# Two blocks of a transformer: large tiles in SBUF moved to multiples of 128 bytes

## The chip, the cores and the metric

The kernel runs on one core of a Trainium2 chip. The metric is the time of one execution in device microseconds; a median of several runs is given. The profile is of one further execution.

## What is computed

Two different blocks are applied one after the other to one sequence of 256 tokens with a width of 2048, all in fp32. The reference, cut to its products:

```python
def first_block(x, ...):
    h = rms_norm(x, norm1_w[l])
    proj = h @ w_in[l]                          # 2048 x 10792
    o_nsa = nsa_mixer(q, nsa_kv, nsa_g, ...)    # sparse attention, 8 heads
    o_dn = gated_deltanet(dn_qkv, dn_z, ...)    # 8 heads, chunks of 64
    mixed = g_nsa * (o_nsa @ w_up_nsa[l]) + g_dn * (o_dn @ w_up_dn[l])
    x = x + mixed @ w_o[l]
    h2 = rms_norm(x, norm2_w[l])
    x = x + (silu(h2 @ w_ffn_gate[l]) * (h2 @ w_ffn_up[l])) @ w_ffn_down[l]
    return rms_norm(x, norm_f_w)

def second_block(x, ...):
    h = rms_norm_2(x, attn_norm_g[l])
    proj = h @ w_in[l]
    y_rwkv = rwkv7_mixer(h_r, h_k, h_v, ...)    # a recurrence over the tokens
    y_mla = mla_mixer(c_q, c_kv, k_pe, ...)     # latent attention
    x = x + concatenate([y_rwkv, y_mla]) @ w_out[l]
    h = rms_norm_2(x, ffn_norm_g[l])
    x = x + conv_glu_ffn(h, w_gate, w_up, conv_w, conv_b, w_down)
    return rms_norm_2(x, final_norm_g)
```

Both feed-forward blocks are 5632 wide. The weights, 476 MB, are read once.

## The kernel before

Every large product is made of f32r matmuls on operands split in two parts: `hi` is the value rounded to f32r, `lo` the rest. Three products of parts (hi hi, hi lo, lo hi) are added in PSUM. The weights come as pieces of 128 x 1024 numbers (512 KB) into one of five `wraw` buffers (`wchunks`); ScalarE makes `whi` from a piece (line 294) and VectorE `wlo` (line 295), three buffers each. The activations are split once and stay in SBUF.

There are two kinds of product. In `gemm_tok` (token-major) the activation is the stationary operand, 128 tokens at a time, and the weights are the moving one, 512 columns, in a few places 256. `mm3` issues a triple for each k and each half of the tokens: stationary hi with `whi`, stationary hi with `wlo`, stationary lo with `whi`. In `gemm_feat` (feature-major) the weights are stationary and the activation is moving. Its hi and lo parts of 256 tokens each lie behind each other, so that one matmul of 512 columns takes both with `whi`; one of 256 columns takes the hi part with `wlo`. For a piece of four k there are eight wide matmuls and then eight narrow ones.

```python
def mm3(self, o, a, b, start, stop):          # gemm_tok
    self.mm(o, a[0], b[0], start, False)
    self.mm(o, a[0], b[1], False, False)
    self.mm(o, a[1], b[0], False, stop)
...
for k, (wh, wl) in piece:                     # gemm_feat, wide
    for m in range(nm):
        self.mm(ps[:, m].rearrange("p i t -> p (i t)"), wh[:, ms[m]], X.wide(xk0 + k), k == 0, False)
...
for k, (wh, wl) in piece:                     # gemm_feat, narrow
    for m in range(nm):
        self.mm(ps[:, m, 0], wl[:, ms[m]], X[0][:, xk0 + k], False, k == kt - 1)
```

The order of the work is fixed when the program is built: `weave` lays the products and the steps of the mixers beside each other by a table of costs (`Pace`), and the recording helper gives almost every instruction the line 131. So instructions go by their tiles. A row names out<-moving,stationary: `mmA<-whi,se` is a matmul of gemm_tok with the activation `se` stationary, `mmA<-hh,whi` one of gemm_feat with the activation `hh` moving. `pB` is the output of the mixers' small matmuls.

The stages in order of time: block 1's projections and mixers (gemm_feat on `sbc`, the gates `z` with gemm_tok), the gates and products that merge them, `w_o` (gemm_tok on `sbc`), gate and up of the feed-forward block (gemm_feat on `sde`), down (gemm_tok on `sbc`, which then holds the first 16 of 44 k, and on `hidh` and `hidl`); block 2's projections (gemm_feat and gemm_tok on `sde`) with its mixers, the latent attention's projections (`sd`), the output projection (gemm_tok, first on `se`, then on `sa`), gate and up (gemm_feat on `hh`), down (gemm_tok, on `sa` for hi and `se` for lo of the first 16 k, then on `hidh` and `hidl`; the last 512 columns as two groups of 256).

Where a tile lies: tiles are laid out once, when the program is built, pool by pool, from below and, for the pools of the right side, from above. `cpool` (constants) comes first, then `wpool` (weights), `hpool` (slot `sa`), `npool` (small tiles and `xn`), then the pools of the stages. `pad0` and `pad1` are tiles of 32 bytes that nothing reads or writes; `pad0` puts the weights' buffers at multiples of 128 bytes. Within a tile every operand of a large product begins a multiple of 512 bytes behind the tile's start, so it has the tile's remainder.

Of the kernel before, what the change touches and what calls it, by code (L numbers as in the profile page):

```python
# [9 lines left out]
F32 = mybir.dt.float32  # L10
# [8 lines left out]
P = 128  # L19
# [99 lines left out]
class Traced:  # L119


    def __init__(self, pace, key):
        self.pace, self.key, self.eng = pace, key, getattr(pace.nc, key)
# [104 lines left out]
class Kern:  # L228
    def __init__(self, tc, A, out, ctx):
        self.tc, self.nc, self.A, self.out, self.ctx = tc, Pace(tc.nc), A, out, ctx  # L230
        self.cpool = ctx.enter_context(tc.tile_pool(name="cpool", bufs=1))

        self.cpool.tile([P, 8], F32, name="pad0")
        ctx.enter_context(tc.tile_pool(name="rpool", bufs=1, side="right")).tile([P, 8], F32, name="pad1")
        self.wpool = ctx.enter_context(tc.tile_pool(name="wpool", bufs=3))
        self.hpool = ctx.enter_context(tc.tile_pool(name="hpool", bufs=1))
        self.npool = ctx.enter_context(tc.tile_pool(name="npool", bufs=2))
        self.psA = ctx.enter_context(tc.tile_pool(name="psA", bufs=2, space=PSUM))
        self.psB = ctx.enter_context(tc.tile_pool(name="psB", bufs=4, space=PSUM))
        self.ident = self.cpool.tile([P, P], F32, name="ident")  # L240
        self.prm = self.cpool.tile([P, NPARAM], F32, name="prm")
        self.cst = None
        self.sides = ctx.enter_context(ExitStack())
        self.new_side()
        self.later = []
# [1677 lines left out]
```

## Time and profile before

| | before |
|---|---|
| median of 3 runs | 2783.31 us (2782.2 to 2783.56) |
| the profiled execution, its own time | 2780.21 us |
| its span, first to last instruction | 2778.4 us |
| mean granted clock of TensorE | 0.998 |
| TensorE busy | 2733.4 us, 98% |
| VectorE, ScalarE, GpSimd busy | 1828.6, 1334.3, 224.6 us |
| read from HBM | 476.30 MB, 173 GB/s over the span |

A busy time counts an engine as busy from the start of an instruction to its end. TensorE's matmuls are pipelined: one begins long before the last has ended, so what a matmul costs is the distance from its start to the next one's. In a timeline, where equal instructions that follow each other stand in one row, that distance is read from the starts of rows and the counts between them.

### The profile page before, as it was taken

To read this page: it belongs to the slowest core of one execution; us is meant where nothing else is said; L and a number is where in the kernel's file an instruction comes from. 1 tells how busy PE (TensorE), PEld (TensorE's weight loads), DVE (VectorE), ACT (ScalarE), POOL (GpSimd) and SP (SyncE) were. 2 spreads that over 40 slices of the span, in tenths; PEclk is the share of its full clock that TensorE was granted. 3 is DMA by queue.
4 is the path that set the end of the run, shared out by engine and by line. 5 is a ranking of instruction groups with operands and counts; after the bars stand their busy time and mean duration, and the time that the engine had idled before them with its cause. 6 is when DMAs were issued, how large, how long until landed. Compare 5 with 4: busy or idle time off the path is not lost.

```text
span 2778.4 us, 39888 instructions
## 1 busy us (share of the span) xinstructions
PE 2733.4 (98%) x15536; PEld 2342.9 (84%) x15536; DVE 1828.6 (66%) x2590; ACT 1334.3 (48%) x1775; POOL 224.6 (8%) x253
## 2 busy tenths in 40 slices
PE   9999999999999999999999999999999999999998
PEld 8987888888788888888888877878888888888888
DVE  7788769866565565564555787776576677675454
ACT  5556545454454444443444544445354444444433
POOL 0000000001000000000001321110000000000000
PEclk9999999999999999999999999999999999999999
DMA  7643465555656665565555643332556666665554
GB/s 243 205 144 106 130 190 167 173 162 181 218 185 191 193 192 190 190 191 188 192 195 183 199 121 107 109 89 105 199 179 192 190 191 191 193 189 189 188 188 143
DMA packets 418655, 484.15 MB, mean 174 GB/s; under 512 B 26113, under 2 KB 343297, under 8 KB 417826
## 3 DMA queue, kind: packets, MB, share of 16 engines
q1 hardware_dynamic: 415808, 475.94, 53.8%
q10 hardware_dynamic: 2658, 5.66, 0.6%
q8 instruction: 122, 2.00, 0.3%
q14 instruction: 67, 0.55, 0.1%
HBM read 476.30 MB, written 5.24 MB: 173 GB/s over the span
## 4 chain that ended last, share of the span: by engine, by line
PE 87%; DVE 4%; POOL 1%; ACT 1%; issue 1%; DMA 0%; ACTq 0%; DVEq 0%; POOLq 0%
PE mmA L131 78%; PE pB L131 8%; DVE wlo L295 1%; DVE iw L131 1%; POOL sd L131 0%; ACT whi L294 0%; DVE ar L131 0%; DVE sd L131 0%; DVE MM L131 0%; DVE xn L131 0%; DMA wA<-in_rwkv_w_dram 0%; POOL psb L131 0%; POOL xn L131 0%; DVE X L131 0%; DVE bt L131 0%
## 5 line engine op out<-in xcount | busy, mean ns | idle before, releaser
L295 DVE TENSOR_TENSOR wlo<-wraw,whi 128x1024 fp32r<-128x1024 f32 x889 | 1092.9, 1231 | 768.1 <-ACT whi L294 754.0
L294 ACT CAST whi<-wraw 128x1024 fp32r<-128x1024 f32 x889 | 928.1, 1045 | 1168.1 <-PE mmA L131 1001.6
L131 PE MATMUL mmA<-sde,whi 128*128 128x512 f32 (+1 forms) x1888 | 468.2, 387 | 1.1 <-DVE sde L131 1.1
L131 PEld LDWEIGHTS mmA<-sde,whi 128*128 128x128 f32 x1888 | 334.5, 188 | 56.4 <-DVE sde L131 1.3
L131 PE MATMUL mmA<-hh,whi 128*128 128x512 f32 x1408 | 351.8, 392 | 0.0
L131 PE MATMUL mmA<-sbc,whi 128*128 128x512 f32 (+1 forms) x1216 | 304.4, 383 | 2.0 <-ACT whi L294 1.5
L131 PEld LDWEIGHTS mmA<-hh,whi 128*128 128x128 f32 x1408 | 251.5, 188 | 43.2
L131 PEld LDWEIGHTS mmA<-sde,wlo 128*128 128x128 f32 x1840 | 249.2, 188 | 20.4 <-DVE wlo L295 1.7
L131 PE MATMUL mmA<-sde,wlo 128*128 128x256 f32 x1840 | 261.5, 279 | 1.5 <-DVE wlo L295 1.5
L131 PEld LDWEIGHTS mmA<-sbc,whi 128*128 128x128 f32 x1216 | 212.5, 188 | 35.8 <-ACT whi L294 2.6
L131 PE MATMUL mmA<-whi,sbc 128*128 128x512 f32 (+1 forms) x768 | 234.4, 379 | 0.6 <-DVE xn L131 0.6
L131 PEld LDWEIGHTS mmA<-hh,wlo 128*128 128x128 f32 x1408 | 188.2, 188 | 14.6
L131 PE MATMUL mmA<-hh,wlo 128*128 128x256 f32 x1408 | 191.5, 278 | 0.0
L131 PE MATMUL mmA<-whi,hidh 128*128 128x512 f32 (+1 forms) x504 | 186.5, 370 | 0.0
L131 PE MATMUL mmA<-wlo,hidh 128*128 128x512 f32 (+1 forms) x504 | 186.5, 370 | 0.0
L131 PE MATMUL mmA<-whi,hidl 128*128 128x512 f32 (+1 forms) x504 | 186.5, 370 | 0.0
L131 PE MATMUL mmA<-sbc,wlo 128*128 128x256 f32 x1152 | 172.6, 281 | 1.4 <-DVE wlo L295 1.4
L131 PEld LDWEIGHTS mmA<-sbc,wlo 128*128 128x128 f32 x1152 | 158.8, 188 | 14.7 <-DVE wlo L295 1.8
L131 PEld LDWEIGHTS mmA<-whi,sbc 128*128 128x128 f32 x768 | 142.0, 188 | 29.6 <-DVE xn L131 0.8
L131 PE MATMUL mmA<-wlo,sbc 128*128 128x512 f32 (+1 forms) x384 | 144.8, 377 | 0.6 <-DVE wlo L295 0.6
L131 POOL TENSOR_TENSOR sg<-sg,rb 128x512 f32<-128x512 f32 x44 | 68.1, 1547 | 579.2 <-ACT sg L131 579.2
L131 PEld LDWEIGHTS mmA<-whi,hidl 128*128 128x128 f32 x504 | 95.2, 189 | 17.8
(440 smaller groups left out, 3242.9 us busy)
## 6 DMA issues: line engine op xcount, KB each, us to landing
wraw<-in_w_in_dram SPq DMA_DIRECT2D x232, 512.0 KB, 3.5
wraw<-in_w_ffn_gate_dram SPq DMA_DIRECT2D x88, 512.0 KB, 3.4
wraw<-in_w_ffn_up_dram SPq DMA_DIRECT2D x88, 512.0 KB, 3.5
wraw<-in_w_ffn_down_dram SPq DMA_DIRECT2D x88, 512.0 KB, 4.2
wraw<-in_ffn_w_gate_dram SPq DMA_DIRECT2D x88, 512.0 KB, 3.5
wraw<-in_ffn_w_up_dram SPq DMA_DIRECT2D x88, 512.0 KB, 3.6
wraw<-in_ffn_w_down_dram SPq DMA_DIRECT2D x88, 512.0 KB, 3.4
wraw<-in_w_o_dram SPq DMA_DIRECT2D x32, 512.0 KB, 3.6
```

Source lines behind the costliest of these rows:

```text
L131: r = f(out, *a, **k)
L294: nc.nc.scalar.copy(h, r)
L295: nc.nc.vector.tensor_sub(l, r, h.bitcast(F32))
```

## The change

`pad1` grows from 32 to 96 bytes, and a new tile of 64 bytes, `pad2`, stands first in `npool`. Nothing uses either.

```diff
         self.cpool.tile([P, 8], F32, name="pad0")
-        ctx.enter_context(tc.tile_pool(name="rpool", bufs=1, side="right")).tile([P, 8], F32, name="pad1")
+        ctx.enter_context(tc.tile_pool(name="rpool", bufs=1, side="right")).tile([P, 24], F32, name="pad1")
         self.wpool = ctx.enter_context(tc.tile_pool(name="wpool", bufs=3))
         self.hpool = ctx.enter_context(tc.tile_pool(name="hpool", bufs=1))
         self.npool = ctx.enter_context(tc.tile_pool(name="npool", bufs=2))
+        self.npool.tile([P, 16], F32, name="pad2", bufs=1)
```

Everything from `npool` upwards moves up by 64 bytes, everything on the right side moves down by 64. No instruction is added, removed or moved. The start of some tiles in a partition, in bytes, and its remainder by 128, as the two built programs have them:

```
tile                          before            after
wraw, whi, wlo (11 buffers)   19072 ... 60032    the same     0 ->  0
sa                            64128              64128        0 ->  0
xn (3 buffers)                80512 ... 84608    + 64         0 -> 64
sbc, hh                       88256              88320       64 ->  0
hidh                         121024             121088       64 ->  0
hidl                         149696             149760       64 ->  0
se, sde                      196544             196480       64 ->  0
cst (block 1)                121600             121664        0 -> 64
ar, km, bt (block 2)         130560 ... 148992   + 64         0 -> 64
X, XT, Lo, Y (block 2)       159296 ... 173696   + 64        64 ->  0
```

`sa` is 16 KB long. The matmuls of f32r by the remainders of their operands' starts (moving, stationary), counted in the built programs:

```
columns  matmuls  before    after
512      4544     (64, 0)   (0, 0)    gemm_feat, wide
512      2616     (0, 64)   (0, 0)    gemm_tok
512       384     (0, 0)    (0, 0)    gemm_tok on sa
256      5132     (64, 0)   (0, 0)    gemm_feat, narrow, and short ones
256       688     (0, 64)   (0, 0)    gemm_tok, narrow
256       128     (0, 0)    (0, 0)    gemm_tok on sa, narrow
```

Of the fp32 matmuls of the mixers, 375 have a stationary operand that goes from 64 to 0, and 256 one that goes from 0 to 64.

## Rows read from the trace of the kernel before

**Rows 1.** The page: busy time by engine, and TensorE's granted clock in 40 slices.
```profile
PE 2733.4 (98%) x15536; PEld 2342.9 (84%) x15536; DVE 1828.6 (66%) x2590; ACT 1334.3 (48%) x1775; POOL 224.6 (8%) x253
...
PEclk9999999999999999999999999999999999999999
```

**Rows 2.** The page's chain that ended last; waits: who for whom, us, times, longest.
```profile
PE 87%; DVE 4%; POOL 1%; ACT 1%; issue 1%; DMA 0%; ACTq 0%; DVEq 0%; POOLq 0%
...
ACT whi L294 <- PE mmA L131: 1001.6, 633, 8.2
```

**Rows 3.** Stretches: from:to us, busy time by engine (instructions), clock, DMA, GB/s.
```profile
8.00:782.00 774.00, 764.46 (x4475) 652.21 (x4476) 571.50 (x884) 415.66 (x596) 41.20 (x50) 1.00 0.56 174
782.00:1269.00 487.00, 487.00 (x2832) 428.94 (x2831) 288.34 (x296) 233.79 (x271) 39.34 (x22) 1.00 0.60 191
...
1518.00:2034.00 516.00, 494.04 (x2992) 417.93 (x2990) 377.53 (x730) 248.67 (x410) 88.23 (x117) 0.99 0.43 136
...
2521.00:2778.00 257.00, 246.31 (x1320) 210.80 (x1319) 121.37 (x120) 97.49 (x106) 15.09 (x9) 0.99 0.51 176
```

**Rows 4.** Timeline of TensorE, output projection on `se`: start us, us, matmul, count.
```profile
1948.70 0.39 PE L131 MATMUL mmA<-wlo,se 128*128 128x512 f32 x1
1948.94 0.63 PE L131 MATMUL mmA<-whi,se 128*128 128x512 f32 x2
...
1971.81 0.39 PE L131 MATMUL mmA<-wlo,se 128*128 128x512 f32 x1
```

**Rows 5.** Timeline of TensorE, output projection on `sa`.
```profile
1990.63 0.39 PE L131 MATMUL mmA<-wlo,sa 128*128 128x512 f32 x1
...
2010.35 0.39 PE L131 MATMUL mmA<-wlo,sa 128*128 128x512 f32 x1
```

**Rows 6.** Timeline of TensorE, down projection of block 2: mixed triples, then `hidh`, `hidl`.
```profile
2524.72 0.40 PE L131 MATMUL mmA<-whi,se 128*128 128x512 f32 x1
...
2542.75 0.40 PE L131 MATMUL mmA<-whi,se 128*128 128x512 f32 x1
2542.98 0.39 PE L131 MATMUL mmA<-whi,hidh 128*128 128x512 f32 x1
...
2546.48 0.40 PE L131 MATMUL mmA<-whi,hidh 128*128 128x512 f32 x1
```

**Rows 7.** Timeline of TensorE, the same projection's groups of 256 columns, mixed triples.
```profile
2704.96 0.28 PE L131 MATMUL mmA<-whi,sa 128*128 128x256 f32 x1
...
2709.55 0.28 PE L131 MATMUL mmA<-whi,sa 128*128 128x256 f32 x1
```

**Rows 8.** Groups of instructions by shape: count, busy us, mean ns of one, idle before.
```profile
L131 PE MATMUL mmA<-whi,hidh 128*128 128x512 f32 x392 | 155.0, 396 | 0.0
...
L131 PE MATMUL mmA<-whi,sa 128*128 128x512 f32 x224 | 77.4, 390 | 0.0
...
L131 PE MATMUL mmA<-whi,hidh 128*128 128x256 f32 x112 | 31.5, 281 | 0.0
...
L131 PE MATMUL mmA<-whi,sa 128*128 128x256 f32 x64 | 18.0, 281 | 0.0
...
L131 PEld LDWEIGHTS mmA<-whi,hidh 128*128 128x128 f32 x504 | 94.7, 188 | 17.8
...
L131 PEld LDWEIGHTS mmA<-whi,sa 128*128 128x128 f32 x288 | 54.1, 188 | 8.9
```

**Rows 9.** Timeline of TensorE, gate and up of block 2: wide and narrow matmuls in turn.
```profile
2300.28 2.00 PE L131 MATMUL mmA<-hh,whi 128*128 128x512 f32 x8
2302.11 1.07 PE L131 MATMUL mmA<-hh,wlo 128*128 128x256 f32 x8
2303.02 1.99 PE L131 MATMUL mmA<-hh,whi 128*128 128x512 f32 x8
2304.85 1.11 PE L131 MATMUL mmA<-hh,wlo 128*128 128x256 f32 x8
2305.79 0.39 PE L131 MATMUL mmA<-hh,whi 128*128 128x512 f32 x1
```

## Prediction

> **What bounds the kernel now.** I read the page's busy shares first. [...] Second, the chain that ended last: 87% of it is TensorE [rows 2]. Third, who waits for whom: ScalarE's split of the weights waits 1001.6 us in all for TensorE to give a `whi` buffer back [rows 2], so the weights are ahead of TensorE and not behind. Fourth, the stretches: in the gate and up products of the first feed-forward block TensorE has no idle time at all (487.00 of 487.00 us); its idle time lies in the mixers and at the end [rows 3]. So the time is the sum of the distances from the start of one matmul to the start of the next. A row's own duration (some 390 ns for 512 columns) overlaps its neighbours'; only the distance counts.
>
> The change adds, removes and moves no instruction: on every engine the two programs' lists agree word for word but for tile numbers and line numbers, waits included. What differs is where tiles begin. So each term is a number of matmuls times a difference in distance that belongs to an address.
>
> **The token-major products (gemm_tok).** Here the activation is the stationary operand and the weights, which lie at 0 of 128 before and after, are the moving one. The trace of before holds both cases of the stationary operand. In the output projection of block 2, first half, it is `se`, at 64 of 128: from 1948.70 to 1971.81 us there are 33 triples of matmuls, 23.11 us, so 700 ns a triple, 233.4 each [rows 4]. In the second half it is `sa`, the one large tile that lies at 0 of 128: from 1990.63 to 2010.35 us there are 29 triples, 19.72 us, so 680 ns a triple, 226.7 each [rows 5]. Code, weights, width and engines' load are alike in the two halves. In the down projection of block 2 both kinds of tile stand in one triple (two `sa`, one `se`): 18.03 us for 26 triples, 693.5 ns; directly after it `hidh` and `hidl`, both at 64, need 3.50 us for 5, 700 ns [rows 6]. The difference follows the tile and changes within a quarter microsecond, so it is not the stage's.
>
> The count, from the loops: the down projection of block 1 has 4 x 44 x 2 = 352 triples, `w_o` 128, the two `z` gates 64, the two latents 64, the first half of the output projection 64, and the down projection of block 2 3 x 28 x 2 = 168: 840 triples at 700 ns. They go to 680: 840 x 20 ns = **16.8 us less**. The 96 mixed triples go from 693.5 to 680: **1.3 us less**. The down projection's last two groups are 256 columns wide, and there the alignment shows nothing: mixed triples with `sa` take 4.59 us for 13, 353 ns or 117.7 each [rows 7], and the mean duration is 281 ns whether the stationary operand is `sa` or `hidh`, while at 512 columns it is 390 against 396 [rows 8]. The weight loads themselves last 188 ns in either case [rows 8], so the gain is not in the load's length. I cost the narrow ones at nothing.
>
> **The feature-major products (gemm_feat).** Here the weights are stationary, at 0 of 128, and the activation is moving, at 64 of 128 before and at 0 after. No row of before has this product with a moving operand at 0, so I bound it. A stretch of the second feed-forward block shows eight matmuls of 512 columns and then eight of 256, in turn: 1.83 us for the eight wide ones (2300.28 to 2302.11), 228.8 each; 0.91 and 0.94 us for the narrow ones, 113.8 and 117.5 by turns, 115.6 on average [rows 9]. The loops give 4544 wide and 4544 narrow ones (2816 in the feed-forward blocks, 1728 in the mixers).
>
> Wide: the nearest row with both operands at 0 is the `sa` triple, 226.7 [rows 5]. That gives 2.1 x 4544 = 9.5 us less. At the other end nothing changes. I take the row: **9.5 us less**. Narrow: the two levels that stand by turns are the bounds. All at 113.8 would be 1.8 x 4544 = 8.2 us less, all at 117.5 1.9 x 4544 = 8.6 us more. The nearest row with both operands at 0 is the triple of 256 columns, 117.7 [rows 7], so I take the upper one: **8.6 us more**. These two terms nearly cancel, and both are weaker than the first.
>
> **The other operands.** The small fp32 matmuls of the mixers read some tiles that move from 64 to 0 and some that move from 0 to 64 (`cst`, `ar`, `bt`, `km` among them): of their stationary operands 375 go to 0 and 256 leave it. At the 6.7 ns of the wide products that would be 2.5 us less and 1.7 us more; they are 256 columns or narrower with few exceptions, where rows 7 and 8 show no difference, so I take 0. The `xn` tiles move from 0 to 64, read and written by VectorE and ScalarE; these have 34% and 52% of the span free [rows 1], and that slack hides it. If it were gone, TensorE would idle for longer where it waits for these engines now, in the mixers: there it idles 22 us of 516 in block 2 [rows 3]. A faster TensorE asks the weights' transfers for under 1% more; the 1001.6 us of waiting [rows 2] cover that.
>
> **Sum.** 16.8 + 1.3 + 9.5 - 8.6 = 19.0 us less; all but the idle stretches pass it on, so I take 18. The profiled execution took 2780.21 us by its own time, 3.1 under the median of the runs, 2783.31: it would become 2762, and the median 2765. Bounds of this case: 18.1 + 9.5 + 8.2 = 35.8 us less, and 18.1 - 8.6 = 9.5 us less, or 2747 to 2774.
>
> **Rivals.**
> First, `sa` is fast for where it lies and not for its alignment: its 16 KB begin where the weights' buffers end. Then the triples stay at 700 ns, and only the uncertain terms are left, which nearly cancel: about 2783. For it: `sa` is the only large activation at 0, so the trace can't part the two. Against it: the nearest of the slow ones, `hidh`, begins 40 KB behind the end of `sa`, and `se` 113 KB, and both run at 700, so between these two the place makes no difference [rows 4, 6].
>
> Second, no offset counts that is a multiple of something smaller than 64. Then `sa` and `se` would not differ, and the time stays at 2783. Rows 4 to 6 speak against it directly; what is left is that `sa` differs in some way I don't see. [...]
>
> Third, slower: in gemm_feat the two operands now lie at the same phase, where before they lay half of 128 apart, and they may get in each other's way when the next weights load beside the running matmul. If the wide ones then take what a bad pair takes elsewhere, 233.4 instead of 228.8, that is 20.9 us more; with all narrow ones at 117.5, 8.6 more: 29.5 - 18.1 = 11.4 us more, 2795. It decides where a wide and a narrow one together lose more than 18.1 us / 4544 = 4.0 ns. Against it: in the `sa` triples both operands are at 0 too, and those are the fastest rows of this width.
>
> That the change doesn't do what it says can be left out: the built program's addresses show every large activation at 0 of 128.
>
> **Numbers.** My forecast 0.78, the first rival 0.10, the second 0.05, the third 0.07. A measurement of this kernel tells about 0.2% from no change, 5.6 us; the whole range of the forecast is beyond that. So faster 0.78, same 0.15, slower 0.07. The range is the forecast's own, 2747 to 2774, carried up to 2780 to take in the rivals' nearer side.
>
> **What would show it.** Right: triples of 680 ns in both down projections and in `w_o`, wide ones of 226 to 227 ns in gemm_feat, unchanged busy times of VectorE and ScalarE. The first step is wrong if `hidh` triples still take 700 ns; the second if the wide ones of gemm_feat stay at 228.8; the third if the narrow ones go to 113.8 throughout (a larger gain), or beyond 117.5. The forecast is wrong as a whole if TensorE's sum falls and idle time before it grows by as much.

## The result: slower by 0.6%

The changed kernel takes 2799.88 us (median of 5 runs, 2797.68 to 2800.9) against 2782.41 us for the kernel before (5 runs beside them): a ratio of 1.0062, interval 1.0051 to 1.0073. That is 17.5 us more where 18 less were forecast. The two profiled executions stand 20.2 us apart (2780.21 and 2800.45), their spans 20.3 (2778.4 and 2798.7).

The page of the changed kernel, busy times, clock and chain, answers to [rows 1, 2]:

```profile
PE 2756.3 (98%) x15536; PEld 2363.0 (84%) x15536; DVE 1834.4 (66%) x2590; ACT 1334.4 (48%) x1775; POOL 219.5 (8%) x253
...
PEclk9999999999999999999999999999999999999999
...
PE 89%; DVE 3%; ACT 1%; issue 0%; POOL 0%; DMA 0%; ACTq 0%; SPq 0%; DVEq 0%; POOLq 0%
```

TensorE's count of instructions is the same, its mean granted clock nearly so (0.998 before, 0.996 after), and it is busy 22.9 us longer; its idle time fell a little (2778.4 - 2733.4 = 45.0 us before, 2798.7 - 2756.3 = 42.4 after). So nothing waits longer: the matmuls themselves lie further apart. The stretches say where. First the gate and up products of block 2 in the kernel before (busy us and instructions of PE, PEld, DVE, ACT, POOL; then clock, DMA share, GB/s):

```profile
2034.00:2521.00 487.00, 487.00 (x2831) 428.57 (x2830) 343.36 (x435) 234.78 (x275) 30.78 (x42) 1.00 0.60 190
```

Then the changed kernel, the stretches of [rows 3] with the one just shown ahead of the last:

```profile
8.00:789.00 781.00, 773.88 (x4475) 659.68 (x4476) 576.27 (x883) 416.61 (x596) 36.84 (x50) 1.00 0.55 172
789.00:1282.00 493.00, 493.00 (x2829) 433.92 (x2828) 288.20 (x295) 232.48 (x271) 39.28 (x22) 1.00 0.59 188
...
1529.00:2046.00 517.00, 495.69 (x2998) 420.96 (x2996) 378.26 (x731) 248.75 (x410) 87.78 (x117) 0.99 0.43 136
2046.00:2542.00 496.00, 496.00 (x2831) 432.77 (x2829) 344.60 (x435) 234.39 (x276) 30.62 (x42) 1.00 0.59 186
2542.00:2797.00 255.00, 245.55 (x1322) 211.91 (x1321) 121.35 (x120) 97.96 (x106) 15.07 (x9) 0.99 0.52 177
```

The two feed-forward stages of gemm_feat have become longer, block 1's (on `sde`) by 6 us and block 2's (on `hh`) by 9; block 1's projections and mixers (gemm_feat on `sbc`) by 7. Block 2's down projection, gemm_tok, is 1 us shorter: from its first matmul to its last it takes 245.2 us where it took 246.2 (its stretch above ends 1.7 us before the span does, that of [rows 3] 0.4). That is the forecast's sign for gemm_tok, at less than its size, and the opposite sign for gemm_feat.

Single rows show it by tile. TensorE's timeline in the changed kernel, as in [rows 4 to 7]: first and last `wlo` row of unbroken triples on `se`, mixed triples, `hidh` and `hidl`, and mixed triples of 256 columns:

```profile
1960.50 0.40 PE L131 MATMUL mmA<-wlo,se 128*128 128x512 f32 x1
...
1994.54 0.39 PE L131 MATMUL mmA<-wlo,se 128*128 128x512 f32 x1
...
2542.29 0.40 PE L131 MATMUL mmA<-wlo,sa 128*128 128x512 f32 x1
...
2563.41 0.39 PE L131 MATMUL mmA<-wlo,sa 128*128 128x512 f32 x1
2564.11 0.40 PE L131 MATMUL mmA<-wlo,hidh 128*128 128x512 f32 x1
...
2599.65 0.40 PE L131 MATMUL mmA<-wlo,hidh 128*128 128x512 f32 x1
...
2724.61 0.28 PE L131 MATMUL mmA<-wlo,sa 128*128 128x256 f32 x1
...
2734.69 0.28 PE L131 MATMUL mmA<-wlo,sa 128*128 128x256 f32 x1
```

`se`: 50 triples in 34.04 us, 681 ns, 226.9 a matmul, where it was 233.4: as forecast. Mixed: 31 triples in 21.12 us, 681 ns: as forecast. But `hidh` and `hidl`: 51 triples in 35.54 us, 697 ns, 232.3 a matmul. They begin at 0 of 128 just as `se` does, and have gained one nanosecond. The narrow mixed triples went up, from 353 ns to 360 (28 in 10.08 us).

The timeline of gate and up, [rows 9]'s view, in the changed kernel, of block 1 on `sde` and of block 2 on `hh`:

```profile
1000.06 2.00 PE L131 MATMUL mmA<-sde,whi 128*128 128x512 f32 x8
1001.90 1.12 PE L131 MATMUL mmA<-sde,wlo 128*128 128x256 f32 x8
1002.86 2.00 PE L131 MATMUL mmA<-sde,whi 128*128 128x512 f32 x8
...
2311.64 2.02 PE L131 MATMUL mmA<-hh,whi 128*128 128x512 f32 x8
2313.49 1.10 PE L131 MATMUL mmA<-hh,wlo 128*128 128x256 f32 x8
2314.43 2.03 PE L131 MATMUL mmA<-hh,whi 128*128 128x512 f32 x8
2316.30 1.12 PE L131 MATMUL mmA<-hh,wlo 128*128 128x256 f32 x8
2317.26 2.02 PE L131 MATMUL mmA<-hh,whi 128*128 128x512 f32 x8
```

Eight wide ones on `sde` take 1.84 us (230.0 each), eight narrow ones 0.96 (120.0). On `hh` the wide ones take 1.85 and 1.87 us (232.5), the narrow ones 0.94 and 0.96 (118.8). Both are slower than before (228.8 and 115.6), and they differ from each other, though both tiles are at 0 of 128.

What divides the tiles stands in the table of tile starts ahead of the prediction, if it is read modulo 256 and not 128. The weights begin at 19072, 128 above a multiple of 256, in both kernels. Before, `sbc` and `hh` (88256), `hidh`, `hidl` and `se`, `sde` all began 64 bytes behind the weights' phase; `sa` (64128) at the same phase. After, `se` and `sde` (196480) have the weights' phase, distance 0; `sbc`, `hh` (88320), `hidh` (121088) and `hidl` (149760) lie 128 away, half a period. A multiple of 128 can be either. In what follows the **distance** is the start of the activation's operand minus that of the weights' operand, modulo 256.

### The profile page after: what moved, and what is told of

It is laid out like the page before. It is cut to its first block, busy times and chain, and to the rows that moved or that the text cites. A ratio compares the mean times of both kernels' runs of the same rounds, so it can differ in the third digit from the quotient of the medians.

```text
span 2798.7 us, 39888 instructions
## 1 busy us (share of the span) xinstructions
PE 2756.3 (98%) x15536; PEld 2363.0 (84%) x15536; DVE 1834.4 (66%) x2590; ACT 1334.4 (48%) x1775; POOL 219.5 (8%) x253
## 4 chain that ended last, share of the span: by engine, by line
PE 89%; DVE 3%; ACT 1%; issue 0%; POOL 0%; DMA 0%; ACTq 0%; SPq 0%; DVEq 0%; POOLq 0%
PE mmA L131 81%; PE pB L131 8%; DVE wlo L296 1%; DVE iw L131 0%; DVE ar L131 0%; DMA cst<-in_consts_dram 0%; DVE MM L131 0%; ACT whi L295 0%; DVE sd L131 0%; POOL psb L131 0%; POOL xn L131 0%; DVE xn L131 0%; DVE bt L131 0%; DVE X L131 0%; ACT sd L131 0%
## 5 line engine op out<-in xcount | busy, mean ns | idle before, releaser
L131 PE MATMUL mmA<-sde,wlo 128*128 128x256 f32 x1840 | 267.4, 283 | 1.5 <-DVE wlo L296 1.5
L131 PEld LDWEIGHTS mmA<-sbc,whi 128*128 128x128 f32 x1216 | 213.4, 189 | 37.5 <-ACT whi L295 2.3
```

The source lines that it names most:

```text
L131: r = f(out, *a, **k)
```

## Experiments

Theory A: the distance modulo 256 sets the spacing of matmuls, with a price list of its own for each kind of product. Its rivals were that the activation's own place modulo 256 counts (B), that the period is 128, and others that stand with the runs. Every edit is shown, and every ratio given, against the kernel before. "Mean spacing" below is worked out from the trace: over all matmuls of one kind and tile, start to start of the next, where the next one on TensorE has the same width; steps over 280 ns wide or 150 ns narrow are left out, and so is the step from the last matmul of an eight to the first of the next eight, which has another width.

**1. The weights moved as well.** The activations on the left reach distance 0, those on the right 128: the reverse of the change.

```diff
-        self.cpool.tile([P, 8], F32, name="pad0")
+        self.cpool.tile([P, 40], F32, name="pad0")
-        ctx.enter_context(tc.tile_pool(name="rpool", bufs=1, side="right")).tile([P, 8], F32, name="pad1")
+        ctx.enter_context(tc.tile_pool(name="rpool", bufs=1, side="right")).tile([P, 24], F32, name="pad1")
+        self.npool.tile([P, 48], F32, name="pad2", bufs=1)
```

> The changed kernel with pad0 32 words larger (128 bytes) and pad2 32 words larger: the weights and sa go from 128 to 0 of 256, the right side (se, sde, sd) stays at 128 of 256, and the lower activations (sbc, hh, hidh, hidl) stay at 0 of 256. Theory A, the distance between the two operands' starts modulo 256 counts: sbc and hidh triples now have distance 0 and go from 697 to about 681 ns (227 each), se triples now have distance 128 and go from 681 to about 697 (232); in gemm_feat the wide matmuls on hh go from 233.0 to about 230.6 and those on sde from 230.6 to about 233; the time about 2790. Theory B, the activation's own place modulo 256 counts (0 is bad, 128 is good): every distance as in the changed kernel, hidh 232, se 227, hh 233.0, sde 230.6, time 2800.

Measured: 2793.35 us, ratio 1.0038 (1.0025 to 1.0051). Its timeline, `se` and then `hidh`:

```profile
1956.50 0.40 PE L131 MATMUL mmA<-wlo,se 128*128 128x512 f32 x1
...
1994.30 0.40 PE L131 MATMUL mmA<-wlo,se 128*128 128x512 f32 x1
...
2558.72 0.39 PE L131 MATMUL mmA<-wlo,hidh 128*128 128x512 f32 x1
...
2596.12 0.39 PE L131 MATMUL mmA<-wlo,hidh 128*128 128x512 f32 x1
```

54 triples on `se` in 37.80 us, 233.3 a matmul; 55 on `hidh` in 37.40, 226.7. The two have changed places against the changed kernel, and so have gemm_feat's: `hh` now 230.6 wide (mean spacing), `sde` 232.9. The activations on the right start where they do in the changed kernel, to the byte; of the two operands only the weights moved, by 128 bytes. B falls, and so does a period of 128. Nor is a longer period needed: modulo 512 the distance of `hh` in the kernel before is 64 and that of `sde` 320, and their wide matmuls take 228.7 and 228.9.

**2 and 3. The two halves of the change.** `pad1` alone (right side at 0, left at 64), and `pad2` alone (left side at 128, right at 64).

```diff
-        ctx.enter_context(tc.tile_pool(name="rpool", bufs=1, side="right")).tile([P, 8], F32, name="pad1")
+        ctx.enter_context(tc.tile_pool(name="rpool", bufs=1, side="right")).tile([P, 24], F32, name="pad1")
```

> Only pad1 grows (the right side: se, sde, sd at 0 of 128 as in the changed kernel), no pad2. If each tile's own address sets its matmuls' distances (both theories): se and sde matmuls as in the changed kernel (wide gemm_feat 230.6, narrow 118.9, gemm_tok 227), sbc, hh and hid as before (228.8, 115.9, 233.4): wide 2048 x +1.8 and narrow 2048 x +2.9 ns are 9.6 us more, the token-major ones 2.9 us less, so 2789. If instead the small tiles (xn and others in npool) or another engine cost the time, the time is that of before, 2782.

```diff
+        self.npool.tile([P, 16], F32, name="pad2", bufs=1)
```

> Only pad2 (xn, sbc, hh, hidh, hidl move as in the changed kernel), pad1 as before. Both theories: hh and sbc wide 2496 x +4 ns and narrow 2496 x +2.6 ns are 16 us more, hid and sbc token-major 2136 x -1 ns 2 us less, so about 2796; the right side as before (228.8, 115.9, se triples 700 ns). The two halves' costs add up to the whole, 17.5 us. If the loss comes from both together, the two halves do not add up.

Measured: 2786.33 us (1.0012, 1.0002 to 1.0022) and 2795.36 us (1.0046, 1.0031 to 1.0061), against 2782.38 before: 4.0 and 13.0 us more, together 17.0 of the whole change's 17.5. The first was expected at 2789, 2.7 us higher. Each tile has the spacing of its distance, whatever the other side does: `sde` 230.6 in the first and 228.9 in the second, `hh` 228.7 and 233.0. The harm is mostly that of the tiles at 128.

**4 to 6. Other distances.** Left at 192 and right at 32; left at 96 and right at 160; left at 224 alone.

```diff
+        ctx.enter_context(tc.tile_pool(name="rpool", bufs=1, side="right")).tile([P, 16], F32, name="pad1")
+        self.npool.tile([P, 32], F32, name="pad2", bufs=1)
```

> A look at two distances that no run has shown: the lower activations begin 192 behind the weights' phase modulo 256 (0 is sa's), the right side 32 behind. Theory A: the wide gemm_feat matmuls at 192 have a value of their own, not that of 64 (228.8) nor 128 (233.0); were only the distance modulo 128 to count, hh at 192 would equal hh before, 228.8 and 115.7, and hid triples 700 ns. At 32 I expect something between 0 and 64: wide 229 to 231, se triples 681 to 700 ns.

```diff
+        ctx.enter_context(tc.tile_pool(name="rpool", bufs=1, side="right")).tile([P, 48], F32, name="pad1")
+        self.npool.tile([P, 8], F32, name="pad2", bufs=1)
```

> The two distances 96 (lower activations: sbc, hh, hidh, hidl) and 160 (right side: se, sde, sd), to fill the table of distances. Theory A (the distance of the operands' starts modulo 256 sets a matmul's cost): values of their own; by their neighbours 64 and 128, and 128 and 192, wide gemm_feat between 228.8 and 233 ns at 96 and about 232 to 233 at 160, narrow 115.7 to 118.6 and 114 to 118.6, token-major 232 to 233.4 and 230 to 232.4. No value below 228.8 for the wide ones would mean that before stood at the best distance for them. Time 2785 to 2797.

```diff
+        self.npool.tile([P, 40], F32, name="pad2", bufs=1)
```

> The last distance, 224, for the lower activations; the right side as before (64). Wide gemm_feat on hh between the values at 192 (232.3) and 0 (230.6), narrow between 114.1 and 118.9, hid triples between 230.5 x 3 and 227 x 3; sde and se as before, 228.9 and 233.4. If any distance makes wide and narrow together cheaper than 228.8 + 115.7 = 344.5 ns, it is this one or none.

Measured: 2791.18 us (1.0031, 1.0019 to 1.0043), 2814.7 us (1.0114, 1.01 to 1.0128) and 2798.66 us (1.0054, 1.0041 to 1.0068). All three hold misses. The second kernel is slower than the whole range expected, and the slowest of the study. At 32 wide matmuls of gemm_feat were expected at 229 to 231 ns and take 233.3; at 224 they were expected at 230.6 to 232.3 and take 233.2, and triples on `hidh` at 681 to 691.5 ns and take 700. Its timeline in gate and up of block 2, `hh` at 96:

```profile
2306.08 2.03 PE L131 MATMUL mmA<-hh,whi 128*128 128x512 f32 x8
2307.95 1.12 PE L131 MATMUL mmA<-hh,wlo 128*128 128x256 f32 x8
2308.91 2.03 PE L131 MATMUL mmA<-hh,whi 128*128 128x512 f32 x8
```

233.8 wide and 120.0 narrow. At 96 the wide ones lie above both neighbours (228.7 at 64, 233.0 at 128): here prices at distances that have not been run can't be drawn from their neighbours; they have to be measured. With these runs the list is full in steps of 32 bytes. Mean spacing in ns, with the tile it is from:

```
distance  gemm_feat 512  gemm_feat 256  gemm_tok 512      gemm_tok 256
   0      230.6 sde      118.9 sde      227.3 se          120.0 hidh
  32      233.3 sde      116.8 sde      233.3 se          118.3 sd
  64      228.7 hh       115.7 hh       233.4 hidh        117.5 hidh
  96      233.8 hh       119.8 hh       234.3 hidh        118.7 hidh
 128      233.0 hh       118.6 hh       232.3 hidh        118.6 hidh
 160      234.1 sde      117.2 sde      233.3 se          119.5 sd
 192      232.3 hh       114.1 hh       229.2 sbc,        117.5 hidh
                                        230.2 hidh
 224      233.2 hh       118.7 hh       233.4 hidh        116.7 hidh
```

The list is of kernels in which `whi` and `wlo` lie at the same distance; run 8 shows what a difference between them does. Tiles at one distance can still differ a little: at 192 `hidl` takes 231.9. For wide matmuls of gemm_tok 0 is best, by about 2 ns or more; for wide ones of gemm_feat 64, where the kernel before already had them; for narrow ones of gemm_feat 192. The kernel before stood at the best place for 4544 wide matmuls and near the best for 4544 narrow ones, and at one of the bad places for gemm_tok.

**7. The hidden values alone.** The kernel before with 192 bytes ahead of `hidh` and `hidl`, which puts them, and no other large operand, at distance 0.

```diff
+    pool.tile([P, 48], F32, name="padh")
     return tuple(Cat(h, pool.tile([P, KF - KD, T], F32R, name="hid" + n)) for h, n in zip(heads, "hl"))
```

> The kernel of before with one pad of 192 bytes ahead of hidh and hidl, nothing else: the activations that are only ever stationary go to distance 0, all that are moving in gemm_feat stay at 64. Theory A: hid triples 681 ns instead of 700 (1176 matmuls x 6.6 ns = 7.8 us less), the 336 narrow ones 2.3 ns more (0.8 us), all else as before: 2775, ratio 0.9975. Theory B (an activation's own place counts, 0 of 256 bad, 128 good): hidh lies at 128 of 256 here too, so the same. If the gain per matmul is given back elsewhere, 2782.

Measured: 2775.88 us, 0.9974 (0.9965 to 0.9983), 7.3 us less. Its timeline, `hidh`:

```profile
2541.67 0.40 PE L131 MATMUL mmA<-wlo,hidh 128*128 128x512 f32 x1
...
2579.08 0.39 PE L131 MATMUL mmA<-wlo,hidh 128*128 128x512 f32 x1
```

55 triples in 37.41 us, 226.7 a matmul, in tiles that lie far from `sa`. So `sa`'s speed was not that of its place, and the forecast's 20 ns a triple do exist, at the right distance.

**8. `wlo` alone.** The kernel before with 128 bytes between the `whi` and the `wlo` buffers (and 128 more behind them, so that all else keeps its phase). The narrow matmuls of gemm_feat go to 192.

```diff
+        if not self.padded:
+            self.padded = True
+            self.wpool.tile([P, 32], F32, name="padw", bufs=1)
         lo = self.wpool.tile([P, 1024], F32R, name="wlo", bufs=WB[2])
...
+        self.hpool.tile([P, 32], F32, name="padp")
```

> The kernel of before with a pad of 128 bytes between the whi and the wlo buffers and another above them: only wlo changes its phase, to 0 of 256; whi and every activation keep theirs. Theory A: the narrow matmuls now have distance 192 to wlo and go from 115.9 to about 114.1 to 115 (4544 x 1.5 = 7 us less); the wide ones stay at 228.8; in gemm_tok the matmuls with wlo go from distance 64 (233.4) to 192 (about 230), those of sa from 0 to 128: 2 us less. Time about 2774. Theory B (an activation's own place counts): no activation moves by its phase, so the narrow ones stay at 115.9 and the time at 2782.

Measured: 2776.04 us, 0.9974 (0.9964 to 0.9985), 7.1 us less. Its timeline in gate and up of block 2:

```profile
2306.20 2.00 PE L131 MATMUL mmA<-hh,whi 128*128 128x512 f32 x8
2308.03 1.07 PE L131 MATMUL mmA<-hh,wlo 128*128 128x256 f32 x8
2308.95 2.00 PE L131 MATMUL mmA<-hh,whi 128*128 128x512 f32 x8
2310.78 1.07 PE L131 MATMUL mmA<-hh,wlo 128*128 128x256 f32 x8
2311.69 2.00 PE L131 MATMUL mmA<-hh,whi 128*128 128x512 f32 x8
```

The narrow eights take 0.92 and 0.91 us, and the alternation with 0.94 of [rows 9] is gone; the wide ones stay at 1.83. The activations keep their phase here, and so does `whi`; only the weights' low part has another. The time is 2 us above the 2774 expected.

In gemm_tok the run shows something that theory A, with one price for each matmul, does not give. Block 2's output projection on `sa`, which stays at distance 0 to `whi` and is now 128 away from `wlo`:

```profile
1984.93 0.39 PE L131 MATMUL mmA<-wlo,sa 128*128 128x512 f32 x1
...
2023.06 0.39 PE L131 MATMUL mmA<-wlo,sa 128*128 128x512 f32 x1
```

55 triples in 38.13 us, 693 ns a triple, where [rows 5] has 680. Two matmuls at distance 0 and one at 128 would be 686 by the list (226.7 + 232.3 + 226.7). The mean steps are 231.0, 229.9 and 232.7 ns: the two matmuls with `whi`, whose own operands did not move, are slower too. So a list by distance holds where all matmuls of a triple have the same one; in a mixed triple the neighbours count. [rows 6] had shown it already: one `se` beside two `sa` makes 693.5, where a third of the way from 680 to 700 would be 687.

**9. Each product at its own distance.** gemm_feat reads at 64, and what gemm_tok alone reads goes to 0: `hidh` and `hidl`, `w_o`'s input and the first 16 k of block 1's down projection (both in `sbc`, now in a tile 192 bytes longer and read from its 192nd byte on), and `se` in block 2.

```diff
-    def pair(self, which):
+    def pair(self, which, off=0):
+        if which == "bc":
+            t = self.h2.tile([P, KD * 2 * T + 48], F32R, name="sbc", tag="slot_bc")[:, off:off + KD * 2 * T]
+            return Parts(t.rearrange("p (k i t) -> p k i t", k=KD, i=2))
...
-        M = K.pair("bc")
+        M = K.pair("bc", 48)
-        hid = hidden(K, fp, K.pair("bc"))
+        hid = hidden(K, fp, K.pair("bc", 48))
...
+        fp.tile([P, 48], F32, name="padh")
         hid = hidden(K, fp, [K.slot(s, [P, KD, T], F32R) for s in "ae"])
...
+        K.side.tile([P, 48], F32, name="padd")
         o = K.slot("e", [P, 2, 8, T], F32R)
+        K.side.tile([P, 16], F32, name="pade")
```

> The kernel before, with an operand moved only where gemm_tok reads it: w_o's input and the first 16 k of down in block 1 start 192 bytes further inside a larger sbc tile, hidh and hidl 192 bytes further, se of block 2's output projection and hidden values 64 bytes lower. The distance activation minus weights goes from 64 to 0 of 256 for 712 triples and for the se part of the 96 mixed ones; all of gemm_feat stays at 64. Theory A (the distance modulo 256 sets the price of each product by itself, so savings add): hidh, hidl, sbc (down, w_o) and se at 226.5 to 227.3 ns for 512 columns, 712 x 3 x 6.5 ns = 13.9 us less, mixed triples 232.4 to 227.1, 1.5 us less, the groups of 256 columns 2.3 ns dearer, 1 us more: 2768.5 (2765 to 2772). Rival C (the saving of the hidden values alone was all there is, or TensorE's gain is given back as waiting for weights): 2775 to 2777, with idle time of TensorE before whi or wlo grown by 6 us or more.

Measured: 2770.08 us, 0.995 (0.9937 to 0.9964) against 2784.68 before: 14.6 us less where 14.4 were worked out (13.9 + 1.5 - 1). Its timeline, block 1's down projection on `sbc`, and block 2's output projection on `se`:

```profile
1280.09 0.39 PE L131 MATMUL mmA<-wlo,sbc 128*128 128x512 f32 x1
...
1290.29 0.39 PE L131 MATMUL mmA<-wlo,sbc 128*128 128x512 f32 x1
...
1941.74 0.40 PE L131 MATMUL mmA<-wlo,se 128*128 128x512 f32 x1
...
1979.85 0.39 PE L131 MATMUL mmA<-wlo,se 128*128 128x512 f32 x1
```

15 triples in 10.20 us and 56 in 38.11: 226.7 and 226.8 a matmul. gemm_feat keeps 228.7 and 115.7 on `hh`.

**10. The same, and `wlo` at 192 for gemm_feat alone.** The `wlo` tile is 256 bytes longer; gemm_feat's pieces begin 128 bytes into it.

```diff
+    def wsplit(self, raw, view, n, feat=False):
-        lo = self.wpool.tile([P, 1024], F32R, name="wlo", bufs=WB[2])
+        lo = self.wpool.tile([P, 1088], F32R, name="wlo", bufs=WB[2])
+        lo = lo[:, 32 if feat else 0:]
```

> The kernel of the run before this one, and a wlo buffer 256 bytes longer, of which gemm_feat uses the part that begins 128 bytes behind the tile's start. So the narrow matmuls of gemm_feat go from a distance of 64 to 192 of 256, and gemm_tok keeps 0 with whi and wlo alike. Theory A: narrow ones from 115.8 to about 114.1 (hh), 114.5 (sde), 115.3 (sbc), some 6.3 us less than without it: 2762 (2759 to 2766); wide ones unchanged at 228.8. Rival C: no more than 2 us under the run without it.

Measured: 2766.93 us, 0.9935 (0.9922 to 0.9947), 17.8 us under the kernel before and the fastest of all. Against run 9 the median falls by 3.2 us, half of the 6.3 expected and 0.9 us above the range given; the profiled span falls by 5.7 (2768.3 to 2762.6). The narrow ones are where they were expected: 114.1 on `hh`, 114.6 on `sde`, 115.2 on `sbc`. The pages of run 9 and of run 10, busy times:

```profile
PE 2722.7 (98%) x15536; PEld 2345.9 (85%) x15536; DVE 1828.1 (66%) x2590; ACT 1334.7 (48%) x1775; POOL 222.4 (8%) x253
```
```profile
PE 2717.0 (98%) x15536; PEld 2338.2 (85%) x15536; DVE 1826.6 (66%) x2590; ACT 1334.8 (48%) x1775; POOL 225.1 (8%) x253
```

TensorE is busy 5.7 us less, near the 6.3 worked out, and its idle time is the same (2768.3 - 2722.7 = 45.6 us, 2762.6 - 2717.0 = 45.6) and near the 45.0 of the kernel before, so rival C has no support in the trace, in run 9 or here. The spans stand further apart than the medians because the profiled execution of run 10 is the fastest of its five (2764.36 us, the slowest 2767.57), that of run 9 the median of its own.

Part of the shortfall has a place in the trace. The wide matmuls were expected unchanged, and their mean spacing is, but it leaves out the last of each eight, which is followed by a narrow one with `wlo`. That step is 235.8 ns on `hh` in run 10 and 230.4 in run 9, and a whole eight takes 1835 ns against 1831 (171 eights). Over all eights that is 2.2 us back, against 6.8 us won on the matmuls of 256 columns. The same step was 230.4 in the kernel before and 235.8 in run 8. That leaves 4.6 us, and the medians have 3.2; the rest is less than executions of one kernel differ by.

## Why the prediction was wrong

The sign was wrong. TensorE's terms, as forecast and as the trace of the changed kernel has them (number of matmuls by change of mean spacing, so that the last of each eight, left out of the means, is counted as the others):

```
term                      forecast   measured
gemm_tok, 840 triples      -16.8      -4.0   hidh, hidl 1176 x -1.0; sbc 960 x -0.9;
                                             se 192 x -6.1; sde 192 x -4.4
mixed triples               -1.3      -1.2   96 x -12.2 a triple
gemm_feat, wide             -9.5     +13.4   hh 1408 x +4.2; sbc 1088 x +3.5;
                                             sde, se, sd 2048 x +1.8
gemm_feat, narrow           +8.6     +12.5   hh 1408 x +2.8; sbc 1088 x +2.3;
                                             sde, se, sd 2048 x +2.9
gemm_tok, 256 columns        0        +1.2   some 800 x +0.4 to +2.8
sum                        -19.0     +21.9   TensorE's busy time +22.9, span +20.3
```

The median moved by 17.5 us and not by 21.9. On record are 2.6 us of idle time that TensorE lost, and 2.8 us by which the profiled pair stands further apart than the medians (2780.21 is 2.2 under its median, 2800.45 0.6 above its own); in the other direction TensorE's busy time grew 1.0 more than the terms.

**What bounds the kernel: right.** The time is the sum of TensorE's distances and an idle time that moved little (45.0 to 42.4 us); the other engines' slack hid what they gained or lost (VectorE 5.8 us more busy, no term of the span).

**The token-major step failed in one sentence:** "The trace of before holds both cases of the stationary operand", at 0 and at 64 of 128. The rows were read rightly, 700 against 680 ns; the label was not. Two tiles can't tell 128 from 256, or the place of one operand from the distance of two. `sa` shares the weights' phase modulo 256, and that made it fast: run 1 keeps `se` in its new place, moves the weights, and `se` is back at 233.3; run 7 brings `hidh` to the weights' phase and it has `sa`'s spacing, 226.7. Of the 840 triples, all put at 680 ns, only the 128 on `se` and `sde` reached distance 0; the 712 others went to 128 and take 697. The table of the change gave every address; it was read modulo 128 because the change speaks of 128.

**The feature-major wide step failed** where it took "the nearest row with both operands at 0", the `sa` triple, as the price of another kind of product. At distance 0 wide matmuls of gemm_feat take 230.6 ns, not 226.7, and 64, where they stood, is their best place. Moreover more than half of them (2496 of 4544) went to 128. The other end of that bound, "nothing changes", let out a loss altogether; no row excluded one.

**The narrow step** had the right sign, but more by luck than by its reading. The row that it leaned on as one "with both operands at 0", 117.7 [rows 7], is of the other kind of product, and one stationary operand in three is `se`, at 64; with all at distance 0 it is 120.0. Its upper bound, 117.5, was the slower of two levels seen at one distance, and another distance has levels above it (0.96 us for eight, 120.0 each). The same holds for the narrow triples of gemm_tok, put at nothing: 353 ns became 360.

**The other operands: nothing, as taken.** TensorE's idle time in the mixers of block 2 is 21.3 us of 517 (22.0 of 516 in [rows 3]).

**The rivals.** The third had the side and the stage: gemm_feat loses more than the 4.0 ns a pair that were named (4.7 on `sde`, 7.0 on `hh`), and it gave 2795. Its mechanism, operands at the same phase in each other's way, is not what the runs show: the same phase costs gemm_feat less than half a period (230.6 ns wide against 233.0), and it is the best place for gemm_tok (227.3 against 229.2 or more). It also kept the whole gain of gemm_tok. The first rival (`sa` is fast for its place) falls by run 7. The prediction's argument against it was sound but named the wrong tile: the nearest slow one is not `hidh`, 40 KB behind the end of `sa`, but `sbc`, 8 KB behind it, with 700 ns a triple in the trace of before. The second, that 64 and 0 are alike because both are multiples of something smaller, falls too: the starts of all these operands are multiples of 32 bytes, and yet the spacing of gemm_tok's wide matmuls moves by up to 7.6 ns (226.7 at distance 0, 234.3 at 96).

What is not settled is why there is such a period. The price goes with gemm_tok and gemm_feat in different ways (of the distances run, wide ones of gemm_tok are fastest at 0, 227.3 ns, those of gemm_feat at 64, 228.7) though both read one operand from the weights' buffers and one from an activation. No offset finer than 32 bytes was run, and no run was made to part a matmul's own two operands from the weight load that runs beside it; runs 1, 8 and 10 show that the neighbour counts, by 4 to 6 ns.

## What to carry to other kernels

An operand's own alignment can be beside the point: `hidh` begins at 0 of 128 in the changed kernel and in run 7, and takes 232.3 and 226.7 ns. Here the spacing of matmuls goes with the distance between the starts of the moving and the stationary operand, modulo a period larger than the alignment (256 bytes), and the best distance is another for each kind of product (0 for wide ones of gemm_tok, 227.3 ns; 64 for wide and 192 for narrow ones of gemm_feat, 228.7 and 114.1). That list holds among neighbours of the same distance; where they differ, the prices do not simply add (run 8: 693 ns a triple, by the list 686). So from a fast and a slow tile in a trace first write down both operands' addresses modulo several powers of two, see which labels part them, and move the other operand in a test before all tiles are moved. A pad that helps one product can cost another that reads the same buffer (`sde` in the changed kernel: 4.4 ns less in gemm_tok, 1.8 more for wide ones of gemm_feat): give each its own distance, by an offset inside the tile if need be (17.8 us here).

## What the hardware showed beyond that

With gemm_tok at distance 0, 256 columns more cost 226.7 - 120.0 = 106.7 ns, 0.417 ns a column. An estimate that takes this rate for both kinds of product and every distance leaves 13.3 ns a matmul beside the columns at distance 0 (120.0 - 106.7), 19.9 for wide ones at a bad distance (233.3 - 213.4), and 7.1 for the faster level of gemm_feat's narrow ones (113.8 - 106.7, [rows 9]). Counted so, it is this remainder that the address changes. That the rate is the same everywhere was not shown: on `hidh` at distance 64 the two widths are 233.4 - 117.5 = 115.9 ns apart.

The weight loads on `hh` do not show it in their own length. Two groups of the changed kernel's page (count, busy us, mean ns of one, idle before), loads for wide and for narrow matmuls on `hh`, at distance 128:

```profile
L131 PEld LDWEIGHTS mmA<-hh,whi 128*128 128x128 f32 x1408 | 252.3, 188 | 46.4
...
L131 PEld LDWEIGHTS mmA<-hh,wlo 128*128 128x128 f32 x1408 | 191.6, 188 | 16.2
```

188 ns a load, as in [rows 8] and as on `hh` in the kernel before, while the wide matmuls' starts lie 4.2 ns further apart and the narrow ones' 2.8.

Nor is the price that of one matmul alone. In the mixed triples of run 1 (`sa` at distance 0 twice, then `se` at 128) the mean steps are 226.8, 232.5 and 234.2 ns: the second matmul has both its own operands at 0 and is slow all the same, with `se` to be loaded next. In runs 8 and 10 the last of eight wide matmuls has its own operands where they were and is 5.4 ns slower (235.8 against 230.4), with `wlo` at another distance to be loaded next. That the next load slows the running matmul is a guess of the author's that no run here shows, and it would not be the whole of it: the third step of those triples, 234.2 ns, is slow too, though the load that follows is of `sa`, at 0.
